# Moving the operands that TensorE holds by 0 to 60 bytes inside their buffers

## The chip, the cores and the metric

The kernel runs on one core of a Trainium2 chip. The metric is the device time of one execution in microseconds; the time before is the median of three runs.

## The reference, cut to what matters

One decoder block over 1024 tokens of width 1024, all in float32. A combined input projection feeds two groups of heads: eight heads of stick-breaking attention (width 64) and four heads of gated DeltaNet (width 128). Each group's output is normalised and gated, and one output projection adds both halves to the residual.

```python
h = rmsnorm(x, norm1_w[layer])
proj = jnp.einsum('btd,de->bte', h, w_in[layer])
# ... attention heads from sb_q, sb_k, sb_v; DeltaNet heads from g_q, g_k, g_v, g_b, g_a ...
mixed = jnp.concatenate([o_sb, o_gdn], axis=-1)
x = x + jnp.einsum('bte,ed->btd', mixed, w_out[layer])
return rmsnorm(x, final_norm_w)
```

## The kernel before

**Split products.** The matmuls of the large products read operands of the type F32R. To keep the precision of float32, each operand is split into a high part (a rounding copy on ScalarE) and a low part (the difference, on GpSimd or VectorE), and a product is made of three matmuls: high with high, high with low, low with high. `mm3` issues these three. The first argument of a matmul is the *held* operand (128 x 128, loaded ahead of the matmul by a weight load), the second is the *moving* operand (128 partitions x up to 512 columns).

**The stages with such products.**
- The q projection, at the start: for each of eight blocks k of the model width, four slices of `wqh` and `wql` are held, and `xh`, `xl` (the input, split) move, 512 columns at a time: 8 k x 8 results x 3 matmuls.
- The value projection: `xh` and `xl` are held and the tiles `chl` move. The change doesn't touch it.
- The projections by column (class `Columns`): 24 columns of 128 outputs for k, for the DeltaNet inputs and for the gates. A column's weights come in two halves of 128 x 512 (`wer`), each split into `weh` and `wel` with three buffers each; a slice of 128 x 128 is held while `xh` or `xl` moves: 24 columns x 2 halves of the tokens x 8 blocks k x 3 matmuls, 512 columns each.
- The output product: per block b of 128 tokens and half g (1 is DeltaNet, 0 is attention), `split` turns the gated block and makes `mh` and `ml` (held); the output weights `woh0` to `woh7` and `wol0` to `wol7` move. Products of the DeltaNet half use the weights 4 to 7, those of the attention half 0 to 3. Sixteen tiles, each with 4 k x 2 x 3 matmuls; the last attention block cuts its second half of the columns into 320 and 192.

**Where tiles lie.** The allocator rounds each tile up to a multiple of 32 bytes per partition and packs the tiles of a pool in the order of their first use; pools on the right side grow down from the end. In the kernel before, taken modulo 64 bytes: `xh`, `xl`, `wqh`, `wql`, `weh` and `wel` all start at 32; `mh`, `ml` and the weights 4 to 7 start at 0; the weights 0 to 3 start at 32. Slices within a tile are 512 or 2048 bytes apart and so keep these numbers. The pools of the projection and of the DeltaNet stage leave less than 200 bytes between them.

**The order of work.** A planner inside the program (`Model`, `interleave`) simulates the engines with costs that depend on an operation's kind and shape, and fixes the order on every engine by it; addresses don't enter. The projections by column are the filler: between 160 and 521 us they run in pieces of 3 to 12 matmuls between those of attention and DeltaNet; before, around 330 us and after 521 us in long runs.

**Small tiles of the DeltaNet stage.** `gdn_pre` runs eight times (4 heads x 2 halves). It makes, on GpSimd, the small tiles `nk` (for ScalarE's scaled copies into `nkv`) and `mr2b` (for VectorE's products into `dt`), each 128 x 4. The scratch tile `yj` takes the squares of the last normalisation, which nobody reads.

Nearly all operations are issued through one recording helper, line 358; the profile's rows are told apart by their tiles.

Of the kernel before, what the change touches and what calls it, by code (L numbers as in the profile page):

```python
# [10 lines left out]
F32 = mybir.dt.float32  # L11
F32R = mybir.dt.float32r
I32 = mybir.dt.int32
AF = mybir.ActivationFunctionType
ALU = mybir.AluOpType
AX = mybir.AxisListType

P = 128
# [24 lines left out]
GAP = "gap"  # L43

PORT = 60


def _rsqrt(V, pool, y, a, n, tag):
# [425 lines left out]
def block(tc, xT_d, x_d, n1_d, wE_d, wQ_d, wC_d, conv_d, alog_d, dtb_d, mixw_d, wo_d, fnw_d, out_d):  # L474
    nc = tc.nc
    ck = Model({"V": nc.vector, "A": nc.scalar, "G": nc.gpsimd, "P": nc.tensor, "S": nc.sync})
    V, A, G, TE, S = ck.V, ck.A, ck.G, ck.P, ck.S

    with ExitStack() as top:
# [80 lines left out]

        class Columns:


            def __init__(self, e):
                self.e, self.raw, self.hl = e, [], []
# [9 lines left out]
            def split(self):  # L575
                ck.prio, prio = WEIGHTS, ck.prio
                r = self.raw[len(self.hl)]
                h = pr.tile([P, 4, P], F32R, tag="weh", bufs=3, name="weh")
                l = pr.tile([P, 4, P], F32R, tag="wel", bufs=3, name="wel")
                hf = h.rearrange("p k e -> p (k e)")  # L580
                A.activation(hf, r, AF.Copy)
                G.tensor_tensor(l.rearrange("p k e -> p (k e)"), r, hf.bitcast(F32), ALU.subtract)
                self.hl.append((h, l))
                ck.prio = prio

        def mm3(out, lh, ll, rh, rl, start, stop):
# [48 lines left out]
        raw, loads = [], {}  # L635
        for k in range(NK):
            w = s0.tile([P, 512], F32, tag="wcr", bufs=6, name="wq")
            wh = s0.tile([P, 512], F32R, tag="wqh", bufs=2, name="wqh")
            wl = s0.tile([P, 512], F32R, tag="wql", bufs=2, name="wql")
            xr = fx.tile([P, T], F32, f"xr{k}", "kq") if k < 4 else s0.tile([P, T], F32, name=f"xr{k}")  # L640
            raw.append(xr)
            lows = []
            for part, u, n in (("w", 0, 1), ("x", 0, 1)) if k else (("x", 0, 2), ("w", 0, 2), ("w", 1, 2), ("x", 1, 2)):
                size = (T if part == "x" else 512) // n
                es = slice(u * size, (u + 1) * size)
                if part == "w":
                    dma = S.dma_start(w[:, es], wQ_d[:, k, es])
                    if k == 0 and u == 0:
                        V.tensor_copy(wh[:, es], w[:, es])
                    else:  # L650
                        A.activation(wh[:, es], w[:, es], AF.Copy)
                    lows.append(V.tensor_tensor(wl[:, es], w[:, es], wh[:, es].bitcast(F32), ALU.subtract))
                else:
                    dma = S.dma_start(xr[:, es], xT_d[k * P:(k + 1) * P, es])
                    A.activation(xh[:, k, es], xr[:, es], AF.Copy, scale=n1[:, k:k + 1])
                    split = [xr[:, es], n1[:, k:k + 1], xh[:, k, es].bitcast(F32), ALU.mult, ALU.subtract]
                    if k or u:
                        V.scalar_tensor_tensor(xl[:, k, es], *split)
                    else:
                        first_split = split  # L660
                if k == 0 and part == "w" and u == 0:
                    later(V.scalar_tensor_tensor(xl[:, 0, 0:512], *first_split), lows[0])
                loads.setdefault(f"k{k}", []).append(dma)
            if k:
                loads[f"k{k}"].reverse()
            if k:
                for j in range(8):
                    i, hs = j // 2, slice((j % 2) * 512, (j % 2) * 512 + 512)
                    es = slice(i * P, (i + 1) * P)
                    mm3(qp[j], wh[:, es], wl[:, es], xh[:, k, hs], xl[:, k, hs], False, k == NK - 1)  # L670
                continue
            for pair in ((0, 2), (4, 6), (1, 3), (5, 7)):
                for a, (lw, rx) in enumerate(((wh, xh), (wl, xh), (wh, xl))):
                    for j in pair:
                        TE.matmul(qp[j], lw[:, (j // 2) * P:(j // 2) * P + P], rx[:, 0, (j % 2) * 512:(j % 2) * 512 + 512], start=a == 0, stop=False)
# [336 lines left out]
        def gdn_pre(h, g):  # L1012
            st = gst[h, g]
            kq = st["kq"]
            cs = slice(4 * g, 4 * g + 4)
            kn = gd.tile([P, 4, P], F32, tag="kn", bufs=4, name="kn")
            ss = gd.tile([P, 2, 4], F32, tag="ss", name="ss")
            cb = gd.tile([P, 4, P], F32, tag="cb", name="cb")
            S.dma_start(cb, cum_s[1, h, cs].partition_broadcast(P))
            dt = gd.tile([P, 4, P], F32, tag="dt", bufs=4, name="dt")  # L1020
            S.dma_start(dt, dt_s[h, g])

            nkv = gd.tile([P, 4, P], F32, tag="nkv", bufs=4, name="nkv")
            kw = fx.words(kq, "kw")
            for which in range(2):
                tp = pz()
                for j in range(4):
                    TE.transpose(tp[:, j * P:(j + 1) * P].bitcast(F32R), kw[:, j, which, :], idr)
                for j in range(4):
                    A.activation(nkv[:, j, :], tp[:, j * P:(j + 1) * P], AF.Square, accum_out=ss[:, which, j:j + 1])  # L1030
                sq = [("A", 250)] * 4
                if which == 0:
                    V.tensor_copy(kn.rearrange("p c d -> p (c d)"), tp)
                    yield
            G.tensor_scalar(ss, ss, EPS, None, ALU.add)
            r2b = gd.tile([P, 4], F32, tag="r2b", bufs=4, name="r2b")
            V.reciprocal(r2b, ss[:, 0, :])
            G.tensor_tensor(r2b, r2b, gsc["beta"][:, h, cs], ALU.mult)
            mr2b = gd.tile([P, 4], F32, tag="mr2b", name="mr2b")
            r = G.tensor_scalar(mr2b, r2b, -1.0, None, ALU.mult)  # L1040
            r2k = gd.tile([P, 4], F32, tag="r2k", bufs=4, name="r2k")
            G.tensor_tensor(r2k, r2b, gsc["kd"][:, h, cs], ALU.mult)
            nk = gd.tile([P, 4], F32, tag="nk", name="nk")
            G.tensor_tensor(nk, ss[:, 0, :], root, ALU.pow)
            qe = gd.tile([P, 4], F32, tag="qe", bufs=4, name="qe")
            G.tensor_scalar(qe, ss[:, 1, :], EPS * P, None, ALU.mult)
            yield r
            nm = dt
            at = gd.tile([P, 4, P], F32, tag="at", bufs=4, name="at")
            for i in range(2):  # L1050
                gpt = pz()
                for j in range(2):
                    c = 2 * i + j
                    TE.matmul(gpt[:, j * 256:(j + 1) * 256], kq[:, c, 0, :], kq[:, c, :, :].rearrange("p a t -> p (a t)"),
                              start=True, stop=True)
                gv = gpt.rearrange("p (j a t) -> p j a t", j=2, a=2)
                V.tensor_tensor(at[:, 2 * i:2 * i + 2, :], gv[:, :, 1, :], dt[:, 2 * i:2 * i + 2, :], ALU.mult)
                for j in range(2):
                    c = 2 * i + j
                    r = V.scalar_tensor_tensor(nm[:, c, :], gpt[:, j * 256:j * 256 + P], mr2b[:, c:c + 1], dt[:, c, :], ALU.mult, ALU.mult)  # L1060
                yield
            st.update(kn=kn, qe=qe, r2b=r2b, r2k=r2k, nkv=nkv, nm=nm, at=at)
            flags[f"p{2 * h + g}"] = r
            yield from until(f"v{2 * h + g}g")
            vt = st["vt"]
            tp = pz()
            for j in range(4):
                TE.transpose(tp[:, j * P:(j + 1) * P].bitcast(F32R), vt[:, j, :], idr)
            for j in range(4):
                A.activation(nkv[:, j, :], tp[:, j * P:(j + 1) * P], AF.Copy, scale=nk[:, j:j + 1])  # L1070
            qg = kq[:, :, 1, :]
            flags[f"q{2 * h + g}"] = G.tensor_tensor(qg, qg, cb, ALU.mult)
            yield
# [293 lines left out]
        pools = {}  # L1367
# [37 lines left out]
            mg = fx.tile([P, 2, 512], F32, "mg", "kq")  # L1405
            return mg, mg[:, 0, :], mg[:, 1, :].rearrange("p (k t) -> p k t", k=4)

        def split(pool, mg, gt):
            tp = pz()
            mw = fx.words(mg, "mw")  # L1410
            yield from turned(tp, [mw[:, 0, j * P:(j + 1) * P] for j in range(4)])
            fv = pools[0].tile([P, 512], F32, tag="mf", name="mf")
            V.tensor_tensor(fv, tp, gt.rearrange("p k t -> p (k t)"), ALU.mult)
            ck.free(mg)
            mh, ml = [pool.tile([P, 4, P], F32R, tag=f"m{c}", bufs=3, name=f"m{c}") for c in "hl"]
            A.activation(mh.rearrange("p k t -> p (k t)"), fv, AF.Copy)
            r = G.tensor_tensor(ml.rearrange("p k t -> p (k t)"), fv, mh.rearrange("p k t -> p (k t)").bitcast(F32), ALU.subtract)
            ck.hold(mh, ml)
# [33 lines left out]
        def prepare(g):  # L1452
            for b in range(NB):
# [1 line left out]
                mg, gt, r = ready["in", b, g]  # L1455
                yield r
                yield lambda: ps.room("pz", 4)
                ready[b, g] = yield from split(pools[0], mg, gt)
                yield

        def product(b, g, parts):
# [51 lines left out]
        def products_attention():  # L1513
            yield lambda: f"d{NB - 1}" in flags
            for b in range(NB):
# [3 lines left out]
                for got in product(b, 0, parts):  # L1519
# [5 lines left out]
                        sy = pools[0].tile([P, 3], F32, tag="sy", bufs=2, name="sy")  # L1525
                        yf = block_tile(0, "yf") if last else y
                    V.tensor_tensor(y[:, hs], yp, y[:, hs], ALU.add)
                    junk = pools[1].tile([P, 512], F32, tag="yj", name="yj")
                    if n == 2:
                        V.scalar_tensor_tensor(junk[:, 0:hs.stop - hs.start], y[:, hs], 1.0 / D, y[:, hs], ALU.mult, ALU.mult, accum_out=sy[:, n:n + 1])  # L1530
                    else:
# [77 lines left out]
```

## Time and profile before

| | |
|---|---|
| median of 3 runs | 650.76 us (650.74 to 650.8) |
| the profiled execution | 650.36 us |
| its span, first to last instruction | 648.4 us |
| mean granted clock of TensorE | 0.997 |
| TensorE busy | 639.2 us, 99% of the span, 3976 matmuls |
| weight loads busy | 549.7 us, 85% |
| VectorE, ScalarE, GpSimd busy | 423.4, 393.7, 341.4 us |
| DMA | 111.82 MB, mean 172 GB/s |

How to read the rows: PE is a matmul on TensorE and PEld a weight load, which overlaps it. In a group, `pp<-xh,weh` names the result and both operands, `x360` the count, then the busy time in us and the mean duration of one in ns, then the idle time before. Matmuls are pipelined, so their durations overlap; the distance of their starts is what they cost. In the chain of work that ended last, a piece gives its start in us, its length in us, its engine, the result tile and the number of instructions. A row of the windows begins with the stretch, then its length, the busy time and the count of the instructions asked for, the granted clock, the DMA share and GB/s.

### The profile page before, as it was taken

The numbers are of one execution on the slowest core, as the hardware profiler recorded it, in microseconds if no ns is written. First come the engines' busy times: TensorE is split into PE (matmuls) and PEld (weight loads), VectorE is DVE, ScalarE is ACT, GpSimd is POOL, SyncE is SP. The second block draws the span as 40 slices with busy tenths as digits, with TensorE's granted clock in tenths as the row PEclk, the third lists the DMA queues.
The fourth block names the chain that finished last, engine by engine and source line by source line (L and its number), as shares of the span: only waits on it lengthen the run. The fifth ranks groups of instructions, "written<-read, shape, count | busy, mean of one in ns | idle before, by whom it ended". The sixth has DMA issues, their size and how long they took to land.

```text
span 648.4 us, 11679 instructions
## 1 busy us (share of the span) xinstructions
PE 639.2 (99%) x3976; PEld 549.7 (85%) x3976; DVE 423.4 (65%) x779; ACT 393.7 (61%) x945; POOL 341.4 (53%) x428
## 2 busy tenths in 40 slices
PE   8999999999999999999999999999999999999996
PEld 7889989988888898888988878888888888888885
DVE  4469974223877869888528887457874326568874
ACT  6664577724967779876559786467854343043553
POOL 0115056837894678835479686287731223226642
PEclk9999999999999999999999999999999999999998
DMA  8976338865383446453463752725312259963312
GB/s 302 324 271 229 133 116 281 285 221 182 106 280 119 129 127 186 133 154 109 121 215 82 263 165 78 225 90 173 109 58 82 82 196 310 346 194 106 123 77 119
DMA packets 96666, 111.82 MB, mean 172 GB/s; under 512 B 28576, under 2 KB 61536, under 8 KB 96608
## 3 DMA queue, kind: packets, MB, share of 16 engines
q1 hardware_dynamic: 96320, 110.89, 52.4%
q8 instruction: 31, 0.51, 0.3%
q14 instruction: 27, 0.22, 0.1%
q10 hardware_dynamic: 288, 0.20, 0.1%
HBM read 76.03 MB, written 35.03 MB: 171 GB/s over the span
## 4 chain that ended last, share of the span: by engine, by line
PE 91%; DVE 4%; issue 1%; ACT 1%; POOL 1%; DMA 1%; POOLq 0%; SPq 0%; DVEq 0%; ACTq 0%
PE pp L358 55%; PE pz L358 26%; PE po L358 7%; PE pc L358 3%; DVE cc L358 1%; DMA kqf<-g_s 1%; ACT sgf L358 0%; DVE al L358 0%; DVE pp L358 0%; POOL sgf L358 0%; DVE wy L358 0%; DVE xr L358 0%; DVE ac L358 0%; POOL wel L358 0%; POOL ac L358 0%
## 5 line engine op out<-in xcount | busy, mean ns | idle before, releaser
L358 PE MATMUL pp<-xh,weh 128*128 128x512 f32 x360 | 150.3, 417 | 0.0
L358 PE MATMUL pp<-xh,wel 128*128 128x512 f32 x360 | 141.5, 393 | 0.0
L358 PE MATMUL pp<-xl,weh 128*128 128x512 f32 x360 | 141.0, 392 | 0.0
L358 POOL TENSOR_TENSOR wel<-wer,weh 128x512 fp32r<-128x512 f32 x48 | 62.8, 1314 | 86.1 <-ACT weh L358 69.7
L358 POOL TENSOR_TENSOR sgf<-sgf,cc 128x128 f32<-128x128 f32 (+3 forms) x64 | 77.3, 1210 | 50.4 <-DVE cc L358 45.0
L358 PEld LDWEIGHTS pp<-xh,wel 128*128 128x128 f32 x360 | 67.6, 188 | 15.2
L358 PEld LDWEIGHTS pp<-xl,weh 128*128 128x128 f32 x360 | 67.9, 189 | 8.6
L358 PEld LDWEIGHTS pp<-xh,weh 128*128 128x128 f32 x360 | 67.7, 188 | 8.7
L358 ACT ACTIVATE sgf<-pz,rs 128x384 f32<-128x384 f32 (+3 forms) x96 | 54.9, 606 | 7.5 <-PE pz L358 7.4
L358 DVE TENSOR_TENSOR_SCAN cc<-pz,step 128x384 f32<-128x384 f32 (+2 forms) x64 | 53.6, 847 | 8.9 <-ACT pz L358 7.4
L358 DVE TENSOR_TENSOR al<-pz,ah 128x512 fp32r<-128x512 f32 (+1 forms) x80 | 49.4, 628 | 13.3 <-ACT ah L358 12.9
L358 ACT ACTIVATE ah<-pz 128x512 fp32r<-128x512 f32 (+1 forms) x80 | 44.4, 572 | 21.0 <-PE pz L358 20.8
L358 ACT ACTIVATE pz<-pz,ns 128x384 f32<-128x384 f32 (+3 forms) x96 | 54.4, 585 | 0.0
L358 PE MATMUL pp<-woh,mh 128*128 128x512 f32 (+2 forms) x132 | 52.1, 394 | 0.0
L358 PE MATMUL pp<-woh,ml 128*128 128x512 f32 (+2 forms) x132 | 51.1, 387 | 0.0
L358 PE MATMUL pp<-wol,mh 128*128 128x512 f32 (+2 forms) x132 | 51.0, 386 | 0.0
L358 DVE SCALAR_TENSOR_TENSOR pp<-pre,conv,pp 128x512 f32<-128x512 f32 x42 | 31.5, 750 | 20.7 <-ACT pp L358 20.3
L358 POOL TENSOR_TENSOR ml<-mf,mh 128x512 fp32r<-128x512 f32 x16 | 22.1, 1380 | 41.2 <-ACT mh L358 35.6
L358 POOL TENSOR_TENSOR ac<-ac,pre 128x512 f32<-128x512 f32 x24 | 31.0, 1292 | 23.3 <-ACT pre L358 13.5
L358 PE MATMUL po<-ah,v2a 128*128 128x256 f32 (+1 forms) x160 | 41.9, 287 | 0.0
L358 DVE TENSOR_TENSOR_SCAN cc<-pz,cc,step 128x512 f32<-128x512 f32 (+1 forms) x32 | 38.8, 1212 | 2.8 <-ACT pz L358 2.4
L358 PE MATMUL po<-al,v2a 128*128 128x256 f32 (+1 forms) x160 | 38.8, 280 | 0.0
(292 smaller groups left out, 1591.8 us busy)
## 6 DMA issues: line engine op xcount, KB each, us to landing
wer<-wE SPq DMA_DIRECT2D x48, 256.0 KB, 3.8
xr<-x SPq DMA_DIRECT2D x16, 512.0 KB, 8.8
g_s<-ac SPq DMA_DIRECT2D x24, 256.0 KB, 2.5
v_s<-v2e SPq DMA_DIRECT2D x16, 256.0 KB, 2.7
kqf<-g_s SPq DMA_DIRECT2D x16, 256.0 KB, 5.3
v2a<-v_s SPq DMA_DIRECT2D x8, 512.0 KB, 5.0
q<-qk_s SPq DMA_DIRECT2D x8, 512.0 KB, 3.8
kh<-qk_s SPq DMA_DIRECT2D x8, 512.0 KB, 5.2
```

Of the source, the lines that this page charges most:

```text
L358: ins = f(*args, **kw).ins
```

## The change

Each held tile of a split gets a buffer that is larger by 8 words (`weh`, `wel`) or 16 words (`wqh`, `wql`, `mh`, `ml`), and the 512 words that are used start some words into it: 0 to 28 bytes in the first case, 0 to 60 in the second. The number comes from the table `SHIFTS`, by the column's number, the block k, or the number 2b + g of the output tile; the high and the low part of a tile use the same number. The scratch tile `yj` grows by 96 bytes, which moves the tiles of its pool, the weights 0 to 3 among them, down by that much. `mr2b` and `nk` become two rows of one tile, which saves 32 bytes of the DeltaNet pool. No instruction is added or removed.

```diff
+SHIFTS = (0, 4, 8, 12, 1, 2, 6, 14, 3, 5, 7, 9, 10, 11, 13, 15)
+
+
+def shifted(pool, dtype, n, room=16, **kw):
+
+    t = pool.tile([P, 512 + room], dtype, **kw)
+    at = SHIFTS[n % 16] % room
+    return t[:, at:at + 512]
...
         class Columns:
 
+            count = 0
...
             def split(self):
                 ck.prio, prio = WEIGHTS, ck.prio
                 r = self.raw[len(self.hl)]
-                h = pr.tile([P, 4, P], F32R, tag="weh", bufs=3, name="weh")
-                l = pr.tile([P, 4, P], F32R, tag="wel", bufs=3, name="wel")
-                hf = h.rearrange("p k e -> p (k e)")
+                hf = shifted(pr, F32R, Columns.count, 8, tag="weh", bufs=3, name="weh")
+                lf = shifted(pr, F32R, Columns.count, 8, tag="wel", bufs=3, name="wel")
+                if self.hl:
+                    Columns.count += 1
                 A.activation(hf, r, AF.Copy)
-                G.tensor_tensor(l.rearrange("p k e -> p (k e)"), r, hf.bitcast(F32), ALU.subtract)
-                self.hl.append((h, l))
+                G.tensor_tensor(lf, r, hf.bitcast(F32), ALU.subtract)
+                self.hl.append([t.rearrange("p (k e) -> p k e", k=4) for t in (hf, lf)])
...
-            wh = s0.tile([P, 512], F32R, tag="wqh", bufs=2, name="wqh")
-            wl = s0.tile([P, 512], F32R, tag="wql", bufs=2, name="wql")
+            wh = shifted(s0, F32R, k, tag="wqh", bufs=2, name="wqh")
+            wl = shifted(s0, F32R, k, tag="wql", bufs=2, name="wql")
...
-            mr2b = gd.tile([P, 4], F32, tag="mr2b", name="mr2b")
+            few = gd.tile([P, 2, 4], F32, tag="few", name="few")
+            mr2b, nk = few[:, 0, :], few[:, 1, :]
...
-            nk = gd.tile([P, 4], F32, tag="nk", name="nk")
...
-        def split(pool, mg, gt):
+        def split(pool, mg, gt, n):
...
-            mh, ml = [pool.tile([P, 4, P], F32R, tag=f"m{c}", bufs=3, name=f"m{c}") for c in "hl"]
+            mt = [pool.tile([P, 528], F32R, tag=f"m{c}", bufs=3, name=f"m{c}") for c in "hl"]
+            at = SHIFTS[n]
+            mh, ml = [t[:, at:at + 512].rearrange("p (k t) -> p k t", k=4) for t in mt]
...
-                ready[b, g] = yield from split(pools[0], mg, gt)
+                ready[b, g] = yield from split(pools[0], mg, gt, 2 * b + g)
...
-                    junk = pools[1].tile([P, 512], F32, tag="yj", name="yj")
+                    junk = pools[1].tile([P, 536], F32, tag="yj", name="yj")
```

## The prediction

> **What bounds the kernel now.** The page of the profile first: busy shares and the chain that ended last.
>
> ```profile
> PE 639.2 (99%) x3976; PEld 549.7 (85%) x3976; DVE 423.4 (65%) x779; ACT 393.7 (61%) x945; POOL 341.4 (53%) x428
> ...
> PE 91%; DVE 4%; issue 1%; ACT 1%; POOL 1%; DMA 1%; POOLq 0%; SPq 0%; DVEq 0%; ACTq 0%
> ```
>
> TensorE is busy 639.2 of 648.4 us, and 91% of the chain is TensorE. Its order is written out by a planner whose costs know shapes, not addresses, so this change leaves the order alone. A nanosecond more per matmul is therefore a nanosecond of the end, wherever it falls: the sum is a count of matmuls times a change of their spacing. The groups by line give the counts.
>
> ```profile
> L358 PE MATMUL pp<-xh,weh 128*128 128x512 f32 x360 | 150.3, 417 | 0.0
> ...
> L358 PE MATMUL pp<-woh,mh 128*128 128x512 f32 (+2 forms) x132 | 52.1, 394 | 0.0
> ```
>
> The means there (417, 394 ns) overlap one another and are no spacing. The spacing comes from the starts in the timeline, and it shows when the next weights are read.
>
> ```profile
> 75.00 0.39 PE L358 MATMUL pp<-xh,weh 128*128 128x512 f32 x1
> 75.01 0.19 PEld L358 LDWEIGHTS pp<-xl,weh 128*128 128x128 f32 x1
> 75.23 0.39 PE L358 MATMUL pp<-xl,weh 128*128 128x512 f32 x1
> 75.23 0.19 PEld L358 LDWEIGHTS pp<-xh,wel 128*128 128x128 f32 x1
> ```
>
> Matmuls start about 0.23 us apart, and within 0.01 us of each start the load of the next held slice begins, for 0.19 us. So TensorE reads two SBUF streams at once: 512 moving words and 128 held words. The change moves the second stream against the first and touches nothing else of size.
>
> Next, whether distance matters at all. Distance here is the start of the moving operand minus that of the held one, modulo 64 bytes. By the layout before it is 0 for the whole projection and for the DeltaNet half of the output product, and 32 bytes for the attention half. The chain in order of time has both kinds:
>
> ```profile
> 24.98 2.04 PE pz L358 x9
> ...
> 30.42 2.04 PE pz L358 x9
> ...
> 84.01 5.44 PE pp L358 x24
> ...
> 303.13 2.08 PE pp L358 x9
> ...
> 510.04 1.40 PE pp L358 x6
> ...
> 560.22 5.55 PE pp L358 x24
> ...
> 607.25 5.67 PE pp L358 x24
> ```
>
> Undisturbed runs at distance 0 cost 5.44/24 = 226.7 ns a matmul (the q projection too: 24.98 to 30.42 is 24 matmuls). Short pieces between other work, at the same distance 0, cost 2.08/9 = 231 and 1.40/6 = 233 ns: after each interruption the stream takes some matmuls to settle. The output product in pieces of 24 behind four transposes costs 231.3 ns in the DeltaNet half (distance 0) and 236.3 in the attention half (distance 32): 5.0 ns more. The timeline of a long attention stretch, from one group of three to the same place ten groups on (30 matmuls), gives its settled spacing:
>
> ```profile
> 630.18 0.40 PE L358 MATMUL pp<-wol,mh 128*128 128x512 f32 x1
> ...
> 637.18 0.40 PE L358 MATMUL pp<-wol,mh 128*128 128x512 f32 x1
> ```
>
> 7.00/30 = 233.3 ns against 226.7. I take it that the distance makes these 6.6 ns; that something else of that half does is a rival below.
>
> **The change, part by part.** The counts: q projection 8 x 8 x 3 = 192, of which the 24 of k = 0 keep shift 0, so 168 change. Projections by column: 24 x 16 x 3 = 1152. Output: 2 x 192. How many of the 1152 stand in long runs, the windows of the tile weh tell (two of three matmuls hold weh; the column 1.00 is the granted clock):
>
> ```profile
> 72.00:160.00 88.00, 52.64 (x170) 1.00 0.68 224
> 160.00:327.00 167.00, 71.02 (x216) 1.00 0.49 145
> 327.00:339.00 12.00, 10.51 (x35) 1.00 0.71 231
> 339.00:521.00 182.00, 90.00 (x273) 1.00 0.41 127
> 521.00:549.00 28.00, 23.74 (x76) 1.00 0.80 270
> ```
>
> Times 1.5: some 420 in the long runs (170 + 35 + 76) and some 730 in the two interleaved stretches (216 + 273).
>
> The new distances, worked out from the code. A column tile is now 2080 bytes, an odd multiple of 32, so its three buffers alternate by 32 bytes, and weh and wel of the same index differ by 32. With shift 0 (four of the 24 columns) one of the two therefore lies at 32, so no column keeps distance 0 throughout. Four columns are 16 bytes off, sixteen at 4, 8, 12, 20, 24 or 28 bytes. The q tiles and the output tiles keep their bases modulo 64 and take the bare shift. The 96 bytes put the attention half's weights at a multiple of 64, so its distances too are bare shifts: of the 16 output tiles one stays at 0 and one, in the attention half, at 32; the rest lie at distances that no row of this trace shows.
>
> For those the nearest rows are the two settled spacings, 226.7 and 233.3. I take the middle, 230.0, since distance is circular and 0 and 32 are its two opposite points; the bounds are given after the sum.
> 1. q projection: 168 x 3.3 ns = +0.55 us.
> 2. Projections in long runs: 420 x 3.3 = +1.4 us.
> 3. Projections in short pieces: they pass through unsettled spacings already (231 and 233 ns) and are nearer to the worse row, so I add 1 ns: 730 x 1 = +0.7 us.
> 4. DeltaNet half: eight pieces from 5.55 to the middle of 5.55 and 5.67: 8 x 0.06 = +0.5 us.
> 5. Attention half: eight pieces from 5.67 to the same middle: -0.5 us.
>
> Parts with one answer: the split itself is the same copy on ScalarE and subtraction on GpSimd, of the same shapes, written some bytes further; both stand outside the chain's large shares, so even some per cent more there cost nothing. The shared tile for mr2b and nk makes the write of mr2b wait for the readers of the last unit's nk as well. But GpSimd writes nk ahead of mr2b, and behind the same readers:
>
> ```profile
> 398.75 1.04 POOL L358 TENSOR_TENSOR nk<-ss,root 128x4 f32<-128x4 f32 x1
> ...
> 400.36 0.22 POOL L358 TENSOR_SCALAR mr2b<-r2b 128x4 f32<-128x4 f32 x1
> ```
>
> So that wait has ended 1.6 us before; if the planner turned the two round, wel and the solve's subtractions would queue behind it on GpSimd, for at most a microsecond in eight units. The tiles behind in that pool, the delta state and its operands among them, move by 32 bytes: some 290 passes of 128 columns. At 5 ns either way that is 1.4 us either way; no row shows such a pass at another distance, and I take nothing. The scratch tile that grows is only written.
>
> Sum: 0.55 + 1.4 + 0.7 + 0.5 - 0.5 = +2.65 us. The profiled execution took 650.36 us (a span of 648.4 and 2.0 around it), so 653.0; the median of the runs, 650.76, lies 0.4 above the profiled one: **653.4 us**.
>
> Bounds over the 1,700 matmuls, each nanosecond of their mean being 1.7 us. If every distance settled at 233.3 and the short pieces went to the 236 of the attention pieces: 168 x 6.6 + 420 x 6.6 + 730 x 4 + 8 x 120 = +7.8 us, 658.5. If all settled at 226.7 at once, short pieces too: 730 x -5.3, DeltaNet 8 x -110, attention 8 x -230 = -6.6 us, 644.2. Further down lies the one stream here that reads moving words more slowly under the same loads:
>
> ```profile
> 314.87 1.03 PE L358 MATMUL pz<-kqf 128*128 128x256 f32 x4
> ...
> L358 PE MATMUL pz<-kqf 128*128 128x256 f32 x64 | 15.4, 381 | 0.0
> ```
>
> Four passes in 1.03 us, the last of them 0.38 long: 0.65/3 = 217 ns apart. All 1,700 at 217 would be some 25 us less, 626; it is the far end, a price for no conflict at all.
>
> **Rivals.**
> *Faster: distance 0 is itself a collision.* Two streams that start on the same offset in the same moment may meet line by line; 226.7 is still 10 ns above the 217 of the slower stream. If most other distances kept them apart, the mean would fall. It decides from a mean below some 229.5 ns, today's over all 1,700 (590 at 226.7, 730 at some 231, 192 at some 228 and 192 at 233). At a mean of 225 it gives -4.5 x 1.7 = -7.7 us: 643. For it: 32 bytes changed something, so the pattern isn't flat. Against: the only move off 0 that the trace has made it worse, and settled runs at 0 are the best spacing of this kind in it.
>
> [...]
>
> *No change: distance is not the cause.* The attention half could be slower by its other work, and then nothing moves: 650.8. Against: the two halves in the windows of TensorE (DeltaNet first; the last two columns are the DMA share and GB/s):
>
> ```profile
> 578.00:588.00 10.00, 10.00 (x46) 1.00 0.76 231
> 608.00:613.00 5.00, 5.00 (x26) 1.00 0.26 105
> ```
>
> DMA is less busy in the slower half, and the settled spacing of 233.3 holds over 7 us without an interruption. [...] A related case ends at the same time: only 32 is bad and the others are like 0. Then the half with woh0 to woh3 gains up to 8 x 0.12 = 1.0 us and the column tiles 32 bytes apart give some of it back.
>
> **How the numbers follow.** A measurement can tell about 0.2%, 1.3 us, from no change. The forecast (a mix of spacings between the two known ones, 651.5 to 656.5) has 0.50; much slower 0.13; faster by the collision 0.20; no change or a balance 0.17. A tail of the forecast falls within 1.3 us, and a tail of the balance beyond it, on either side. Together: faster 0.22, same 0.17, slower 0.61. The range leaves out the lower half of the faster case and the upper half of the much slower one, 0.17 in all: 645 to 660. The forecast's own range is 651.5 to 656.5.
>
> **What would show it.** The long runs of the chain (24 in 5.44 us) should read between 226.7 and 233.3 ns a matmul and differ from column to column; the q projection's period of 5.44 us should hold for the first k only and lengthen by some 0.08; DeltaNet pieces should come to 5.55 to 5.67 and attention pieces below 5.67, the first attention block lowest. Order and counts on TensorE should be the same, and no new wait on GpSimd. I am wrong if columns off a 16-byte line fall below 226.7, if they exceed 236, or if all read as before.

## The result and the profile after

The changed kernel takes 658.5 us, the median of four runs (657.32 to 659.09), against 650.75 for the kernel before: a ratio of 1.012, interval 1.0107 to 1.0133. It is slower by 7.75 us, where 2.65 were forecast. The direction and the range (645 to 660) held; the size was off by a factor of three. That the time lies in the range is partly luck: as the experiments show, more than half of the cost comes from what the forecast did not count.

The profiled execution after took 659.09 us, with a span of 657.2. Its page, first the busy shares and the chain by engine, then the group of the projections' first product:

```profile
PE 645.0 (98%) x3976; PEld 550.0 (84%) x3976; DVE 425.8 (65%) x779; ACT 395.7 (60%) x945; POOL 334.3 (51%) x428
...
PE 93%; issue 2%; POOL 1%; DVE 1%; ACT 1%; DMA 1%; SPq 0%; POOLq 0%; ACTq 0%; DVEq 0%
...
L368 PE MATMUL pp<-xh,weh 128*128 128x512 f32 x360 | 150.7, 419 | 2.4 <-DVE zt L368 2.4
```

The recording helper is now line 368. The count of matmuls is the same (3976), as is that of every other operation; what came on top are 22 instructions that only wait for semaphores (11701 rows in all against 11679). Two things grew. TensorE is busy for 645.0 us where it was busy for 639.2, +5.8. And the part of the span in which it is not busy grew from 648.4 - 639.2 = 9.2 to 657.2 - 645.0 = 12.2 us, +3.0. The group's last column says where most of that came from: 2.4 us ahead of a projection matmul, where the row of before has 0.0. The view of TensorE's waits (total, times, longest) has six rows that were not there. The three longest:

```profile
PE pp L368 <- DVE zt L368: 2.4, 1, 2.4
...
PE pp L368 <- POOL wel L368: 0.6, 1, 0.6
PE pz L368 <- DMA mgf<-gate_s: 0.4, 1, 0.4
```

So this is not only a change of spacing. The chain in order of time has the spacing, in the pieces that answer to those shown before, and one piece that is neither:

```profile
25.19 2.07 PE pz L368 x9
...
84.81 5.55 PE pp L368 x24
...
548.99 12.99 PE pp L368 x48
...
562.27 5.65 PE pp L368 x24
...
609.74 5.65 PE pp L368 x24
```

The q projection goes from 2.04 to 2.07 for nine matmuls (later blocks to 2.11), a long run from 5.44 to 5.55 for 24 (231.3 ns each), the DeltaNet half from 5.55 to 5.65, and the attention half from 5.67 to 5.65. The piece at 548.99 takes 271 ns a matmul. The windows of TensorE around it (length, busy time and count, granted clock, where 1.00 is full speed, DMA share, GB/s) show what goes with it:

```profile
546.00:549.00 3.00, 0.64 (x4) 1.00 0.59 176
549.00:552.00 3.00, 3.00 (x8) 0.57 0.90 277
552.00:555.00 3.00, 3.00 (x13) 0.86 0.19 73
```

TensorE stands still until 548.99, and then the granted clock is at 0.57 for three microseconds. In the timeline of that place the starts lie 0.42 us apart in the middle of it:

```profile
548.99 0.50 PE L368 MATMUL pp<-xh,weh 128*128 128x512 f32 x1 [2.36 <-DVE zt L368]
...
550.12 0.63 PE L368 MATMUL pp<-xh,weh 128*128 128x512 f32 x1
550.54 0.63 PE L368 MATMUL pp<-xl,weh 128*128 128x512 f32 x1
```

The order of GpSimd changed too. The prediction showed `nk` ahead of `mr2b` there, in another unit; both are `few` now, and the row that reads `ss` and `root` (nk, 1.05 us) comes behind the one that reads `r2b` (mr2b):

```profile
115.80 0.22 POOL L368 TENSOR_SCALAR few<-r2b 128x4 f32<-128x4 f32 x1
115.98 0.20 POOL L368 TENSOR_TENSOR r2k<-r2b,kd 128x4 f32<-128x4 f32 x1
116.14 1.05 POOL L368 TENSOR_TENSOR few<-ss,root 128x4 f32<-128x4 f32 x1
```

Behind that the order of every engine differs from the one before: in the traces, the matmuls that TensorE runs differ in kind from the 629th of the 3976 on, and 202 of the 463 transfers of the DMA queue stand in another place.

### The profile page after: what moved, and what is told of

Read it like the earlier page. It is cut to its first block, busy times and chain, and to the rows that moved or that the text cites. A ratio compares the mean times of both kernels' runs of the same rounds, so it can differ in the third digit from the quotient of the medians.

```text
span 657.2 us, 11701 instructions
## 1 busy us (share of the span) xinstructions
PE 645.0 (98%) x3976; PEld 550.0 (84%) x3976; DVE 425.8 (65%) x779; ACT 395.7 (60%) x945; POOL 334.3 (51%) x428
## 4 chain that ended last, share of the span: by engine, by line
PE 93%; issue 2%; POOL 1%; DVE 1%; ACT 1%; DMA 1%; SPq 0%; POOLq 0%; ACTq 0%; DVEq 0%
PE pp L368 55%; PE pz L368 27%; PE po L368 7%; PE pc L368 3%; DMA mgf<-gate_s 1%; POOL tt L368 1%; DVE xr L368 0%; ACT nkv L368 0%; DVE wol L368 0%; POOL ml L368 0%; POOL wel L368 0%; ACT woh L368 0%; SPq L368 0%; POOL rsg L368 0%; DVE mgf L368 0%
## 5 line engine op out<-in xcount | busy, mean ns | idle before, releaser
L368 PE MATMUL pp<-xl,weh 128*128 128x512 f32 x360 | 142.6, 396 | 0.0
L368 POOL TENSOR_TENSOR wel<-wer,weh 128x512 fp32r<-128x512 f32 x48 | 58.2, 1218 | 95.3 <-ACT weh L368 95.0
L368 POOL TENSOR_TENSOR ml<-mf,mh 128x512 fp32r<-128x512 f32 x16 | 20.2, 1264 | 44.0 <-ACT mh L368 44.0
L368 ACT ACTIVATE weh<-wer 128x512 fp32r<-128x512 f32 x48 | 30.7, 641 | 13.7 <-PE pp L368 7.4
```

The costliest lines, as they stand in the source:

```text
L368: ins = f(*args, **kw).ins
```

## The experiments

Means of spacing below are worked out from the starts in each kernel's timeline: the distance of two successive matmuls of 512 columns, pairs further apart than 245 ns left out. "Long runs" and "short pieces" are the prediction's.

**1. Two prices: the order alone, the spacing alone.** `few_only` is the kernel before with nothing but the shared tile:

```diff
-            mr2b = gd.tile([P, 4], F32, tag="mr2b", name="mr2b")
+            few = gd.tile([P, 2, 4], F32, tag="few", name="few")
+            mr2b, nk = few[:, 0, :], few[:, 1, :]
...
-            nk = gd.tile([P, 4], F32, tag="nk", name="nk")
```

> The kernel before with one edit: mr2b and nk share a tile. No held operand is shifted. The planner's order on every engine is then that of the changed kernel, since the shared tile lets nk be computed only after mr2b. Theory A (two prices: the order, and the spacing of the matmuls): the starts of the 512-column matmuls account for about +4.0 us of the changed kernel's +7.8 (q projection 192 x 4.4 ns, long runs 420 x 4.8, short pieces 730 x 1.0, DeltaNet half 192 x 3.3, attention half 192 x -0.9), so the order alone should cost the rest: 654 to 655.5 us, with TensorE waiting around 530 to 548 us as in the changed kernel, and long runs still at 226.7 ns. Rival B (the spacing makes all of it, and the other order is as good): 650.2 to 651.4 us.

`nkfirst` is the changed kernel, all starts moved, with nk computed ahead of mr2b in the program's text, which gives TensorE, ScalarE, VectorE and the DMA queue the order of the kernel before (six small differences stay on GpSimd):

```diff
+            few = gd.tile([P, 2, 4], F32, tag="few", name="few")
+            mr2b, nk = few[:, 0, :], few[:, 1, :]
+            G.tensor_tensor(nk, ss[:, 0, :], root, ALU.pow)
             r2b = gd.tile([P, 4], F32, tag="r2b", bufs=4, name="r2b")
...
-            few = gd.tile([P, 2, 4], F32, tag="few", name="few")
-            mr2b, nk = few[:, 0, :], few[:, 1, :]
...
-            G.tensor_tensor(nk, ss[:, 0, :], root, ALU.pow)
```

> The changed kernel with one edit: nk is computed ahead of mr2b in the program, which gives TensorE, VectorE, ScalarE and the DMA queue the order of the kernel before. All shifts stay. Theory A: only the price of the spacing is left, 654 to 655.5 us; the stretch after 521 us is as in the kernel before, without the waits of the changed one; spacing in long runs 231 to 233 ns. Rival B: 657.5 to 659 us, as the changed kernel.

Measured: few_only 654.54 us (654.07 to 655.78), ratio 1.0068, interval 1.0055 to 1.0081; nkfirst 653.4 (652.94 to 653.71), ratio 1.0045, interval 1.0032 to 1.0058; the kernel before 650.6 beside both. So the order alone costs 3.9 us, inside the range that was expected of two prices, and the spacing alone 2.8, which is 0.6 us below the range expected of it. Their pages show the two kinds of cost apart, few_only (span 652.3) first:

```profile
PE 639.5 (98%) x3976; PEld 548.9 (84%) x3976; DVE 426.9 (65%) x779; ACT 395.7 (61%) x945; POOL 340.8 (52%) x428
```

and nkfirst (span 651.3):

```profile
PE 642.4 (99%) x3976; PEld 549.4 (84%) x3976; DVE 423.2 (65%) x779; ACT 393.9 (60%) x945; POOL 334.5 (51%) x428
```

In few_only TensorE is busy as before (639.5) and not busy for 12.8 us, 3.6 more than before. In nkfirst it is not busy for 8.9 us, as before, and busy for 3.2 more. One change costs by standing still, the other by slower streaming. Together 3.9 + 2.8 = 6.7, that is 657.3 us; the changed kernel's run with the least loss of clock (mean granted 0.999) took 657.32. Its other three ran at 0.994 to 0.996 and took 658.14 to 659.09. In the profiled one the loss is the stretch shown above: from 549.34 to 552.98 nine spacings take 3.64 us where 9 x 0.232 = 2.09 would do, 1.6 us lost. The same is seen without moved starts: of few_only's five runs three at 0.997 to 0.999 took 654.07 to 654.54, two at 0.994 took 655.55 and 655.78. But it is not bound to the new wait. Of 54 executions of the kernel before beside the experiments, whose profiled execution has no such wait, five ran at 0.996 and took 651.52 to 652.36, the others at most 651.08. Five of the nine executions of the changed kernel and few_only ran at 0.996 or less, and 11 of the 122 of all other kernels, the one before included. So the loss is more frequent with the wait; where it fell is known for the one profiled execution alone. Of the 5.8 us by which TensorE is busier in the changed kernel's profiled execution, 3.2 are then spacing and 1.6 the clock; the last 1.0 was not traced to a place.

**2. Is it the distance modulo 64 bytes?** `yj_only` takes the 96 bytes alone, which sets the attention half's weights to distance 0 modulo 64:

```diff
-                    junk = pools[1].tile([P, 512], F32, tag="yj", name="yj")
+                    junk = pools[1].tile([P, 536], F32, tag="yj", name="yj")
```

> The kernel before with one edit: the scratch tile yj grows by 96 bytes, so that the attention half's output weights start at a multiple of 64 like the rest (distance 0); order unchanged. If the distance makes the attention half's 233.3 ns: settled runs of it at 226.7, pieces of 24 in 5.44 to 5.55 us instead of 5.67, in all 192 x 5 to 6.6 ns = 1.0 to 1.3 us less: 649.5 to 649.8 us. If other work of that half makes it: 650.6 to 650.9 us and pieces of 5.67.

`fixed48` adds fixed starts to it, the moving input 48 bytes in and the output's held tiles 16 bytes in:

```diff
-        xh = px.tile([P, NK, T], F32R, name="xh")
-        xl = px.tile([P, NK, T], F32R, name="xl")
+        xh, xl = [px.tile([P, NK * T + 12], F32R, name=n)[:, 12:].rearrange("p (k t) -> p k t", k=NK) for n in ("xh", "xl")]
...
-            mh, ml = [pool.tile([P, 4, P], F32R, tag=f"m{c}", bufs=3, name=f"m{c}") for c in "hl"]
+            mh, ml = [pool.tile([P, 528], F32R, tag=f"m{c}", bufs=3, name=f"m{c}")[:, 4:516].rearrange("p (k t) -> p k t", k=4) for c in "hl"]
```

> The kernel before with yj grown, and one and the same distance of 48 bytes (moving start minus held start, modulo 64) everywhere: xh and xl start 48 bytes into their tiles, mh and ml 16 bytes into theirs; order unchanged. In the changed kernel the q block whose shift gave this distance ran at 226.7 ns for all its 24 matmuls. Theory D (each single distance has a settled spacing of its own, and 48 shares the good one): long runs 226.7 ns, 649.3 to 650.0 us as for yj_only. Rival E (only distance 0 is good, and that q block was an accident of its start): long runs at 230 to 233, 652.5 to 655 us.

Measured: yj_only 650.12 us, ratio 0.9999, interval 0.999 to 1.0008: nothing. The attention half did not move, though it stands at the same distance modulo 64 as the DeltaNet half:

```profile
607.10 5.67 PE pp L358 x24
613.06 5.64 PE pp L358 x24
```

fixed48: 653.02, ratio 1.004, interval 1.0027 to 1.0053, with means of 230.7 in the q projection, 230.5 in long runs, 232.0 in the DeltaNet half and 232.6 in the attention half. Modulo 64 explains neither. (By the layout fixed48 is one distance modulo 64 only; modulo 256 its q projection stands at 176 and 240.) What sets the stages at 226.7 ns apart from the others here is that their distance is 0 modulo 512: `xh`, `xl`, `weh`, `wel`, `wqh` and `wql` all start at 96 modulo 512, and `mh`, `ml` and the weights 4 to 7 at 384. The attention half stood at 224 modulo 512, with the 96 bytes at 128.

**3. A longer period.** Four kernels, all in the order of before. `yj224` grows the scratch tile by 224 bytes, so that the attention half is at 0 modulo 512 as well:

```diff
-                    junk = pools[1].tile([P, 512], F32, tag="yj", name="yj")
+                    junk = pools[1].tile([P, 568], F32, tag="yj", name="yj")
```

> The kernel before with the scratch tile yj grown by 224 bytes in place of 96, so that the output weights 0 to 3 start 0 bytes from the held tiles modulo 512 (224 before, 128 with the 96 bytes of yj_only; all the other large products are 0 modulo 512 already). Order on every engine as before. Theory F (what counts is the distance modulo a period above 64 bytes, at least 128 and at most 512, and only 0 of it settles at 226.7 ns): the eight attention pieces fall from 5.67 to 5.55 us, their mean spacing from 233.3 to some 228.5 ns: 649.6 us, 1.0 less. Theory G (the attention half is slower for another reason, its other work or its weights): 650.6, spacing 232.5 to 233.3.

`pad64` and `pad128` put an unused tile ahead of the moving input, which moves it against all the weights of the projections; the attention half is set to 256 and 64 by `yj`:

```diff
         xl = px.tile([P, NK, T], F32R, name="xl")
+        px.pool.tile([P, 16], F32, name="pad")
...
-                    junk = pools[1].tile([P, 512], F32, tag="yj", name="yj")
+                    junk = pools[1].tile([P, 632], F32, tag="yj", name="yj")
```

(`pad128`: 32 and 552 words.)

> The kernel before with an unused tile of 64 bytes ahead of xl, so that xh and xl move down by 64 bytes: projections and q projection are at distance 448 modulo 512 (0 modulo 64) in place of 0; the value projection, which holds xh and xl, moves by 64 too. yj is grown so that the attention half is at 256 modulo 512 (0 modulo 256). Order as before. Theory F: q projection and long runs from 226.7 to 230.5 to 232 ns, so 190 x 4.5 + 420 x 4.5 + 730 x 1 = +3.5 us, 654, less if the period were 256 and the attention half gained 1.0. If the period were 64 after all (rival of F): 650.6 or below, long runs 226.7.

> The same with 128 bytes: projections and q projection at 384 modulo 512 (0 modulo 128), attention half at 64 modulo 512. Theory F with a period of 256 or 512: q projection and long runs at 230.5 to 232 ns, +3.5 us, 654. With a period of 128: long runs 226.7, 650.6, and the attention half stays at 232 to 233.

`q4` is yj224 with the split weights of the q projection one word into longer buffers:

```diff
-            wh = s0.tile([P, 512], F32R, tag="wqh", bufs=2, name="wqh")
-            wl = s0.tile([P, 512], F32R, tag="wql", bufs=2, name="wql")
+            wh = s0.tile([P, 640], F32R, tag="wqh", bufs=2, name="wqh")[:, 1:513]
+            wl = s0.tile([P, 640], F32R, tag="wql", bufs=2, name="wql")[:, 1:513]
```

> The kernel of yj224 with the split weights of the q projection 4 bytes into buffers of 2560 bytes (a multiple of 512), so that the q projection alone stands at a distance of -4 modulo 512, everything else at 0. Order as before. Theory F, sharp form (only 0 settles): q projection from 226.7 to 230 to 232 ns, 192 x 4.5 = +0.9 us on yj224. Theory F, flat form (a few bytes are still within the good place): q projection 226.7, the time of yj224. [...]

| kernel | distances modulo 512: q and projections / attention half | mean spacing: q, long runs, attention (ns) | us | ratio, interval |
|---|---|---|---|---|
| before | 0 / 224 | 226.8, 227.4, 233.3 | 650.49 | |
| yj224 | 0 / 0 | 227.2, 227.5, 228.4 | 649.56 | 0.9986, 0.9977 to 0.9995 |
| pad64 | 448 / 256 | 233.3, 233.3, 228.4 | 654.53 | 1.0065, 1.0051 to 1.0079 |
| pad128 | 384 / 64 | 232.4, 232.7, 229.4 | 653.1 | 1.0041, 1.0028 to 1.0053 |
| q4 | q 508, projections 0 / 0 | 232.5, 227.5, 228.4 | 650.67 | 1.0004, 0.9995 to 1.0013 |

The pieces of the attention half in the chain, yj224 first and pad64 (256 bytes) second, against 5.67 before:

```profile
606.22 5.55 PE pp L358 x24
612.06 5.60 PE pp L358 x24
```

```profile
611.74 5.57 PE pp L358 x24
617.60 5.57 PE pp L358 x24
```

Both 0 and 256 are good (228.4 ns), 128 (yj_only, pieces of 5.64 to 5.67 us) and 384 (pad128, 232.4 and 232.7 ns) are not: the period is 256 bytes. A move of 64 or 128 bytes (233.3 and 232.7 ns in long runs) costs the projections as much as the changed kernel's scattered starts (232.3 in nkfirst). And 4 bytes already cost the q projection its good spacing: 192 x (232.5 - 227.2) ns = 1.0 us, about the 650.67 - 649.56 = 1.1 of q4 against yj224. A start that is no multiple of 16 bytes is no worse here than one that is: q4, moved by 4 bytes, has 232.5 ns, pad64, moved by 64, 233.3.

**4. The distances one by one.** In `qscan1` to `qscan3` (q4 with another start for each block k) the q projection walks through a list of distances, 24 matmuls each:

```diff
+            wh = s0.tile([P, 640], F32R, tag="wqh", bufs=2, name="wqh")[:, (0, 63, 60, 56, 48, 40, 64, 8)[k]:(0, 63, 60, 56, 48, 40, 64, 8)[k] + 512]
```

(wql the same; qscan2 has 16, 1, 4, 24, 52, 44, 62, 54 and qscan3 0, 62, 56, 60, 40, 63, 1, 0.)

> The kernel of q4 (attention weights at distance 0, split weights of the q projection in buffers of 2560 bytes), with another start for each of the eight blocks k of the q projection: the distance of moving start minus held start is 0, 4, 16, 32, 64, 96, 256 and -32 bytes modulo 512 for k = 0 to 7, 24 matmuls each. It is read by the mean spacing of the later matmuls of each k, not by its total time (649.5 to 650.7). Period 256, only its 0 good (theory F, sharp): 226.7 ns for k = 0 and 6 alone, 230 to 234 for the others. Period 512: k = 6 at 231 to 233 as well (the attention half of pad64, at 256, spoke against it). If only lags behind the held slice hurt (the attention half of pad128, at +64, lay between): small positive distances, k = 1 to 4, at 226.7 to 229 and k = 7 at 231 to 233.

> The same with distances -64, -4, -16, -96, 48, 80, 8 and 40 bytes for k = 0 to 7. Theory F, sharp: none at 226.7, all 230 to 234, q projection as in q4 (+1.1 us on yj224). If small positive distances are good too: k = 4 to 7 at 226.7 to 229, k = 0 to 3 at 231 to 234.

> The kernel of qscan1 with distances 0, 8, 32, 16, 96, 4, -4 and 0 bytes for k = 0 to 7: 16 and 4, which settled at 226.7 ns when they followed blocks that were settled already, now follow blocks that were not (32 and 96), and 8, which stayed at 233.4 behind an unsettled block, follows distance 0. If the spacing depends on the distance alone: 4 and 16 at 226.7 ns again and 8 at 233.4. If a settled stream is kept within some 16 bytes of distance 0 but not found from there: 8 at 226.7 (or what the stops at the start make of it), 4 and 16 at 231 to 234, and k = 7 at 226.7 after some ten matmuls.

Once per block the chain has a piece of nine matmuls on `pz`. In qscan1, for k = 1 to 7, that is for 4, 16, 32, 64, 96, 256 and -32 bytes:

```profile
14.71 2.04 PE pz L358 x9
...
20.15 2.04 PE pz L358 x9
...
25.67 2.10 PE pz L358 x9
...
31.21 2.06 PE pz L358 x9
...
36.77 2.10 PE pz L358 x9
...
42.33 2.04 PE pz L358 x9
...
47.85 2.10 PE pz L358 x9
```

2.04 is 226.7 ns a matmul, 2.10 is 233.3. In qscan3, for 8, 32, 16, 96, 4, -4 and 0:

```profile
14.66 2.10 PE pz L358 x9
...
20.26 2.10 PE pz L358 x9
...
25.77 2.04 PE pz L358 x9
...
31.30 2.10 PE pz L358 x9
...
36.91 2.10 PE pz L358 x9
...
42.49 2.09 PE pz L358 x9
...
48.04 2.04 PE pz L358 x9
```

Distances 0, 256 and 16 settle at 226.7 in every block that has them (16 does so behind 32, which did not). 4 bytes kept a spacing that was settled (qscan1, behind k = 0) and did not reach it from one that was not (qscan3, behind 96). 8 stays at 233 ns in both scans that have it. Of the others, by the last 14 matmuls of each block, each from its start to the next one's: 64 at 229.6, 80 at 230.5, all the rest, -96, -64, -32, -16, -4, 32, 40, 48, 96, between 231.7 and 234.6. None is below 226.6. It makes no difference which operand moves: pad64 moves the moving one and qscan2's first block the held one, both to -64, and both read 233 ns; at +64, pad128's attention half and qscan1 read 229.4 and 229.6. So the expectation of qscan2 was met but for 234.6 at one distance, and those of qscan1 and qscan3 in part: neither "only 0" nor "the distance alone" nor "kept but not found within 16 bytes" is the whole rule. That the past of the stream counts has a second sign. The changed kernel and nkfirst have the same addresses in the q projection (in block k = 1, by the layout, -16 for the high part and 112 for the low part), and the piece of this block reads, the changed kernel first:

```profile
14.11 2.04 PE pz L368 x9
```

```profile
13.86 2.12 PE pz L368 x9
```

That is 226.7 and 235.6 ns. A figure for a single block of a scan, seen in one execution, is therefore one of the values that its distance can have, and not always the only one. The scans took 650.74, 650.86 and 650.77 us, one run each.

**5. Why the order costs.** The longest new wait is the 2.36 us for VectorE's `zt`. `mf2` is few_only with a second buffer for `mf`, the scratch of the output product's split:

```diff
-            fv = pools[0].tile([P, 512], F32, tag="mf", name="mf")
+            fv = pools[0].tile([P, 512], F32, tag="mf", bufs=2, name="mf")
...
-                    junk = pools[1].tile([P, 512], F32, tag="yj", name="yj")
+                    junk = pools[0].tile([P, 512], F32, tag="mf", bufs=2, name="yj")
```

> The kernel of few_only (the shared tile for mr2b and nk, no operand moved), with two buffers for mf, the scratch of the output product's split, in place of one; to make room the last squares go to the same buffers in place of yj. TensorE's order is that of few_only. Theory A (the order costs by waits of TensorE, the longest 2.36 us ahead of the matmuls at 544 us, where VectorE's zt stands in its queue behind an mf that waits for GpSimd's ml to free the one buffer): that wait goes or shrinks below 1 us, and the time falls from 654.5 to some 652.5. Rival (zt waits for something else: the transposed block, its DMA): the wait stays near 2.4 us and the time at 654.5.

VectorE's timeline in few_only, then in mf2:

```profile
542.20 0.69 DVE L358 TENSOR_TENSOR mf<-pz,mgf 128x512 f32<-128x512 f32 x1 [2.65 <-issue]
544.93 0.69 DVE L358 TENSOR_TENSOR mf<-pz,mgf 128x512 f32<-128x512 f32 x1 [2.04 <-POOL ml L358]
545.54 0.68 DVE L358 TENSOR_TENSOR zt<-pp,zs 128x512 f32<-128x512 f32 x1
```

```profile
541.48 1.29 DVE L358 TENSOR_TENSOR mf<-pz,mgf 128x512 f32<-128x512 f32 x2 [1.89 <-PE pz L358]
542.68 0.68 DVE L358 TENSOR_TENSOR zt<-pp,zs 128x512 f32<-128x512 f32 x1
```

In few_only the second mf waits 2.04 us for GpSimd's ml, which reads the first one out of the only buffer; zt stands behind it in VectorE's queue, and TensorE waits for the buffer of results (pp) that zt reads. The kernel before has the same wait of VectorE, 2.07 us, with zt behind it:

```profile
549.72 0.69 DVE L358 TENSOR_TENSOR mf<-pz,mgf 128x512 f32<-128x512 f32 x1 [2.07 <-POOL ml L358]
550.32 0.68 DVE L358 TENSOR_TENSOR zt<-pp,zs 128x512 f32<-128x512 f32 x1
```

There TensorE had matmuls of the output product to run meanwhile; in the new order its next matmul needs what zt frees. In mf2, with two buffers, both mf run one behind the other, zt follows at 542.68, and TensorE's wait for it is 0.2 us:

```profile
PE pp L358 <- DVE zt L358: 0.2, 1, 0.2
```

mf2 takes 651.71 us (650.79 to 652.47), ratio 1.0012, interval 1.0003 to 1.002, beside 650.85 for the kernel before. Its TensorE order is that of few_only, so some 3 us of the 3.9 came from this one chain. Laid beside few_only matmul by matmul, mf2 gains 0.6 us at 533 us (the wait for `gate_s`, which is gone as well), 2.2 at 546 and 0.4 at 617. The 0.6 us wait for `wel` is still there and makes most of the rest.

## Why the prediction was wrong, point by point

- **"This change leaves the order alone"**: the step that failed. The planner's costs know shapes only, but its dependencies know tiles: a write waits until the first operation recorded on its tile, or on the tile that had the buffer before it, has begun,

```python
                for q in (r, r.prev):
                    if q and q.ops and not q.ops[0].begun:
                        q.ops[0].followers.append(op)
```

  so two small results in one tile are tied in the program's order, mr2b first. "If the planner turned the two round ... at most a microsecond in eight units" named the event and priced it by the delay on GpSimd. The price was elsewhere: the planner laid out everything behind it anew, and the new order has a place (at 544 us in few_only) where one buffer of mf holds up TensorE. +3.9 us where nothing was counted.
- **The loss of clock**: no step of mine had it. It is the 1.2 us between the two prices and the median (657.3 and 658.5), and 1.6 in the profiled execution, there behind the long wait. That the wait causes it is not shown.
- **"Distance modulo 64 bytes"**: wrong. The period is 256, the DeltaNet half and the projections stood at 0 of it, and the attention half at 224, where I took 32 of 64 and "opposite points" of a circle. The two prices that I took from the attention half and from long runs (233.3 and 226.7) were nevertheless near the two ends of what nearly all distances show, and the middle of 230.0 was low: most lie at 231 to 234.6. Modulo 256 the new buffers move the operands too: a q tile of 2112 bytes is 8 x 256 + 64, and a column tile of 2080 is 8 x 256 + 32. So "the 24 of k = 0 keep shift 0" did not mean that they keep their distance: in nkfirst these stand at 64 and 192, by the layout, and end at 232.5 ns, where the prediction had 226.7.
- **The terms.** nkfirst has the order of before, so its trace can be laid beside that of before matmul by matmul, each counted from its start to the next one's:

| step | forecast | before to nkfirst |
|---|---|---|
| 1 q projection | +0.55 | +0.61 |
| 2 long runs | +1.4 | +2.25 |
| 3 short pieces | +0.7 | +0.02 |
| 4 DeltaNet half | +0.5 | +0.60 |
| 5 attention half | -0.5 | -0.11 |
| all other matmuls, taken as 0 | 0 | -0.51 |
| sum | +2.65 | +2.86 |

  The sum of what I took the change to be came out, and that is luck: the rule for the distances was another, and the terms that were missed cancel. Long runs cost more because their mean spacing is 232.3 ns there and not 230. Short pieces cost nothing, as their pieces of 3 to 12 matmuls between other work pass through 231 ns before and 232 after; that the gaps beside them take up the difference was not traced. In the attention half nothing was to be had by 96 bytes. One sum beside the forecast was off as well: all 1,700 at 217 ns, from the prediction's own mean of 229.5, would be 21 us less and not 25. It doesn't move the forecast.
- **The rivals.** "Faster": no distance in the scans is below 226.6 ns. "Much slower", and the "16-byte line" of the prediction's last sentence: no run shows such lines, or a price of starts that are no multiple of 16 bytes; moved by 4 bytes, q4 has 232.5 ns, moved by 64, pad64 has 233.3. The upper end of the range, 660, came close to the measured time for another reason. "No change": the same matmuls at 227.5 and 233.3 ns, by nothing but an unused tile of 64 bytes (yj224 and pad64), decide against it, and in the attention half yj224 does (228.4 ns against 233.3).
- **"No new wait on GpSimd, order and counts on TensorE the same"** was the sign to look for, and it was this that showed the prediction wrong.

## What to carry to other kernels

Before moving an operand for the sake of its address, work out its distance to the other operand of the same matmul modulo 256 bytes: where the large products already stand at 0, every pad ahead of them should keep it so (64 bytes took the long runs from 227.5 ns in yj224 to 233.3 in pad64), and where one does not (the attention half here), a pad of the right size is worth trying: yj224, at 649.56 us, is the fastest kernel of this study, 0.14% below the kernel before (interval 0.05% to 0.23%). In a kernel whose order comes from a planner, putting two small results in one tile is a change of the order (+3.9 us here); compare the written order of every engine before pricing anything else, and price a new order by what stands single-buffered behind it.

## What the runs showed of the hardware that was not expected

- A stream of 512-column matmuls, each behind its own weight load, settled at 226.7 ns after some eight to ten matmuls where the moving start lay 0 modulo 256 bytes from the held one (in the kernel before, from 72.94 us on, the first nine spacings take 2.06 us, 228.9 ns each, and the next twelve 2.72 us, 226.7 each); one pad of 64 bytes made it 233.3 on the mean of the long runs, 2.9% more. The past of the stream counts: 4 bytes kept 226.7 ns in one scan and did not reach it in another, and one block with the same addresses ran at 226.7 and at 235.6 ns in two executions. Which part of the machine has the period of 256 was not found.
- In the changed kernel's profiled execution TensorE stood still for 2.36 us and was then granted half its clock for about 3 us (0.50 from 549.5 to 552.5 us, 0.42 us a matmul). In few_only's profiled execution a stop of the same length was followed by a granted clock of 1.00. Whether the stop brings it, and what decides, wasn't tried; executions of kernels without the stop lose clock as well, though less often (11 of 122 at 0.996 or less, against five of nine).
